# A 3x3 convolution: image pairs held whole, and output rows made in twos from a shared middle product

## The chip, the cores and the metric

The kernel runs on one core of a Trainium2 chip. The metric is device time in microseconds (us) from start to end of one execution. Three runs of the kernel before took 138.09, 137.21 and 137.68 us; the median is 137.68.

## The reference

The input x holds 16 images of 64 channels, 64 x 64 each, in fp32. The weight holds 128 output channels, 64 input channels and 3 x 3 taps; nine tenths of its values are zero, at places that follow no pattern. Each output pixel is the sum over input channels and taps, with a border of zeros around the image:

```python
x_pad = np.pad(x, ((0, 0), (0, 0), (pad, pad), (pad, pad)), mode='constant')
for b, co, ci, kh, kw in ...:
    if weight[co, ci, kh, kw] != 0:
        output[b, co] += weight[co, ci, kh, kw] * x_pad[b, ci, kh:kh+h, kw:kw+w]
```

The output is 16 x 128 x 64 x 64 in fp32, 33.55 MB; the input is 16.78 MB.

## The kernel before, in words

The convolution is done as matrix products: for one tap, the 64 x 128 matrix of its weights (input by output channels) times the pixels of some rows, shifted by the tap. The nine taps of a pixel are added up in one PSUM bank, which holds 512 fp32 values for each of 128 output channels, that is 8 rows of 64 pixels.

A product has only 64 input channels, so it fills half of TensorE's 128 rows of weights. The kernel splits each image: partitions 0 to 63 hold the channels of its upper 33 rows, partitions 64 to 127 those of its lower 33 rows (32 rows and the one that the middle tap row's neighbours need, XROWS = 33). One unit of work is 8 output rows in each half. It takes two PSUM tiles (psum_t, of 8 in the pool) and 18 matmuls, nine taps by two halves, the halves in turn (lines 151 to 181), so that two matmuls on different halves of the array can run beside each other. Pixels beyond the image's edge are left out of the matmul: 63 columns instead of 64 for the side taps, 7 rows instead of 8 at the top and the bottom.

Loads are issued by GpSimd, and they cast fp32 to bf16 on the way. Image 0 comes in four pieces (lines 54 to 60); images 1 to 14 in twos, one transfer for each half (lines 107 to 116), into three buffers, so that a load of a later group waits until TensorE is done with the buffer; image 15 in two transfers (lines 102 and 103).

The weights come by one load on SyncE's queue (line 64), VectorE casts them in three parts (line 70), TensorE multiplies them with an identity (made by GpSimd, line 76) to turn them, and ScalarE copies the result to wT, one 128 x 128 entry for each tap, with the same 64 rows in both halves (lines 79 to 91).

Finished PSUM tiles are copied to SBUF: for images 0 to 12 by VectorE or ScalarE as the planner picks (line 186; in the profile each gets one of the two), for images 13 to 15 by VectorE for the upper and ScalarE for the lower half (lines 188 and 191). Stores are issued by SyncE: images 0, 1 and 12 each by one transfer of 2 MB (line 202), images 2 to 11 in twos, 4 MB each (line 204), and images 13 to 15 in pieces of 512 KB as units finish, SyncE and ScalarE in turn (lines 197 and 199). The order of the instructions on each engine is the planner's, which takes the program's order as its priority.

Of the kernel before, what the change touches and what calls it, by code (L numbers as in the profile page):

```python
# [1 line left out]

# [5 lines left out]

FP32 = mybir.dt.float32  # L10
BF16 = mybir.dt.bfloat16


POS_ORDER = [(1, 1), (1, 0), (1, 2), (0, 0), (0, 1), (0, 2), (2, 0), (2, 1), (2, 2)]
CHUNK_ORDER = [1, 0, 2]


@with_exitstack
def kernel(
# [6 lines left out]
    nc = tc.nc  # L26

    B, C_IN, H, W = x.shape
    C_OUT, C_IN2, KH, KW = weight.shape
    assert (C_IN, H, W) == (64, 64, 64) and (C_OUT, KH, KW) == (128, 3, 3)  # L30

    HALF = H // 2
    XROWS = HALF + 1
    SPLIT = 10

    SINGLE_OUT = {0, 1, 12}
    PAIR_OUT_START = {2, 4, 6, 8, 10}
    STREAM_OUT = {13, 14, 15}
    UNITS_8 = [(r, 8) for r in range(0, HALF, 8)]
    STREAM_UNITS = {  # L40
        13: UNITS_8,
        14: UNITS_8,
        15: [(0, 8), (8, 8), (16, 8), (24, 4), (28, 4)],
    }
# [6 lines left out]
    psum_pool = ctx.enter_context(tc.tile_pool(name="psum", bufs=8, space=bass.MemoryType.PSUM))  # L51

    xs0 = x0_pool.tile([128, XROWS, W], BF16, name="xs0")
    nc.gpsimd.dma_start(out=xs0[0:64, 0:SPLIT], in_=x[0, :, 0:SPLIT, :])  # L54
    nc.gpsimd.dma_start(  # L55
        out=xs0[64:128, 0:SPLIT], in_=x[0, :, H - XROWS : H - XROWS + SPLIT, :]
    )
    nc.gpsimd.dma_start(out=xs0[0:64, SPLIT:XROWS], in_=x[0, :, SPLIT:XROWS, :])  # L58
    nc.gpsimd.dma_start(  # L59
        out=xs0[64:128, SPLIT:XROWS], in_=x[0, :, H - XROWS + SPLIT : H, :]  # L60
    )

    w_sb = const_pool.tile([C_OUT, C_IN * KH * KW], FP32)
    nc.sync.dma_start(out=w_sb, in_=weight.rearrange("o i kh kw -> o (i kh kw)"))
    w_sb3 = w_sb.rearrange("o (i k) -> o i k", k=KH * KW)

    w_bf = const_pool.tile([C_OUT, C_IN * KH * KW], BF16)
    w_bf3 = w_bf.rearrange("o (i k) -> o i k", k=KH * KW)
    for kh in CHUNK_ORDER:
        nc.vector.tensor_copy(  # L70
            out=w_bf3[:, :, kh * KW : (kh + 1) * KW],
            in_=w_sb3[:, :, kh * KW : (kh + 1) * KW],
        )

    ident = const_pool.tile([128, 128], BF16)
    make_identity(nc, ident)

    wT = const_pool.tile([128, KH * KW, C_OUT], BF16)
    for kh in CHUNK_ORDER:
        wps = psum_pool.tile([128, 4, 128], FP32, name="psum_t")  # L80
        for j in range(KW):
            sl = w_bf3[:, :, kh * KW + j]
            for half in range(2):
                nc.tensor.matmul(  # L84
                    wps[half * 64 : (half + 1) * 64, j, :],
                    sl,
                    ident,
                    start=True,
                    stop=True,
                )  # L90
        nc.scalar.copy(out=wT[:, kh * KW : kh * KW + KW, :], in_=wps[:, 0:KW, :])  # L91

    xs_group = None
    oimg_pair = None

    for b in range(B):
        if b == 0:
            xs = xs0
            xsel = ()
        elif b == B - 1:  # L100
            xs = x0_pool.tile([128, XROWS, W], BF16, name="xs15")
            nc.gpsimd.dma_start(out=xs[0:64], in_=x[b, :, 0:XROWS, :])  # L102
            nc.gpsimd.dma_start(out=xs[64:128], in_=x[b, :, H - XROWS : H, :])  # L103
            xsel = ()
        elif b % 2 == 1:
            xs_group = xg_pool.tile([128, 2, XROWS, W], BF16, name="xsg")
            nc.gpsimd.dma_start(  # L107
                out=xs_group[0:64].rearrange("i n r c -> i n (r c)"),
                in_=x[b : b + 2, :, 0:XROWS, :].rearrange("n i r c -> i n (r c)"),
            )  # L110
            nc.gpsimd.dma_start(  # L111
                out=xs_group[64:128].rearrange("i n r c -> i n (r c)"),
                in_=x[b : b + 2, :, H - XROWS : H, :].rearrange(
                    "n i r c -> i n (r c)"
                ),
            )
            xs = xs_group
            xsel = (0,)
        else:
            xs = xs_group  # L120
            xsel = (1,)

        if b in SINGLE_OUT or b in STREAM_OUT:
            oimg = outs_pool.tile([C_OUT, H, W], FP32, name="oimg")
        elif b in PAIR_OUT_START:
            oimg_pair = outg_pool.tile([C_OUT, 2, H, W], FP32, name="oimg2")
            oimg = oimg_pair[:, 0]
        else:
            oimg = oimg_pair[:, 1]

        streamed = b in STREAM_OUT
        if streamed:
            oimg_blk = oimg.rearrange("o (blk r) c -> o blk r c", blk=2)
            out_blk = out[b].rearrange("o (blk r) c -> o blk r c", blk=2)
            units = STREAM_UNITS[b]
        else:
            units = UNITS_8

        for ui, (ur0, rb) in enumerate(units):
            psums = []  # L140
            infos = []
            for half in range(2):
                r0 = half * HALF + ur0
                r1 = r0 + rb
                start_row = 0 if half == 0 else H - XROWS
                pbase = half * 64
                psum_t = psum_pool.tile([128, rb, W], FP32, name="psum_t")
                psums.append(psum_t)
                infos.append((r0, r1, start_row, pbase))

            for idx, (kh, kw) in enumerate(POS_ORDER):
                di, dj = kh - 1, kw - 1
                for half in range(2):
                    r0, r1, start_row, pbase = infos[half]
                    psum_t = psums[half]

                    i_lo = max(r0, -di)
                    i_hi = min(r1, H - di)
                    j_lo = max(0, -dj)
                    j_hi = min(W, W - dj)  # L160

                    rel_lo, rel_hi = i_lo - r0, i_hi - r0
                    xr_lo = i_lo + di - start_row
                    xr_hi = i_hi + di - start_row
                    xc_lo, xc_hi = j_lo + dj, j_hi + dj

                    idx_rhs = (slice(pbase, pbase + 64),) + xsel + (
                        slice(xr_lo, xr_hi),
                        slice(xc_lo, xc_hi),
                    )  # L170
                    rhs = xs[idx_rhs]
                    out_ap = psum_t[:, rel_lo:rel_hi, j_lo:j_hi]
                    lhsT = wT[pbase : pbase + 64, kh * KW + kw, :]

                    nc.tensor.matmul(  # L175
                        out_ap,
                        lhsT,
                        rhs,
                        start=(idx == 0),
                        stop=(idx == len(POS_ORDER) - 1),  # L180
                    )

            if not streamed:
                for half in range(2):
                    r0, r1, _, _ = infos[half]
                    nc.any.tensor_copy(out=oimg[:, r0:r1, :], in_=psums[half])  # L186
            else:
                nc.vector.tensor_copy(  # L188
                    out=oimg[:, infos[0][0] : infos[0][1], :], in_=psums[0]
                )  # L190
                nc.scalar.copy(  # L191
                    out=oimg[:, infos[1][0] : infos[1][1], :], in_=psums[1]
                )
                src = oimg_blk[:, :, ur0 : ur0 + rb, :]
                dst = out_blk[:, :, ur0 : ur0 + rb, :]
                if ui % 2 == 0:
                    nc.sync.dma_start(out=dst, in_=src)
                else:
                    nc.scalar.dma_start(out=dst, in_=src)  # L199

        if b in SINGLE_OUT:
            nc.sync.dma_start(out=out[b], in_=oimg)
        elif (b - 1) in PAIR_OUT_START:
            nc.sync.dma_start(
                out=out[b - 1 : b + 1].rearrange("n o h w -> o n (h w)"),
                in_=oimg_pair.rearrange("o n h w -> o n (h w)"),
            )


# [28 lines left out]
```

## Time and profile before

| what | value |
|---|---|
| median of three runs | 137.68 us |
| span of the profiled execution, first to last instruction | 136.1 us |
| TensorE busy with matmuls | 126.7 us (93%), 1188 of them |
| VectorE, ScalarE, GpSimd busy | 45.2, 40.2 and 12.2 us |
| last matmul ends | 130.5 us |
| read from and written to memory | 17.60 and 33.55 MB |
| TensorE's granted clock | 1.000 |

The profile is of one execution; its span runs from the first to the last instruction on the core, and the time measured for a run contains a little more than that. The page gives no other time of that execution, so its span is set beside the median of the runs. Engines are named PE (TensorE; PEld is its loading of weights), DVE (VectorE), ACT (ScalarE), POOL (GpSimd) and SP (SyncE); a q behind the name means the queue that issues transfers. In a row of the groups of instructions stand the line, the engine, the operation, the tiles written and read, the shapes, the count, then the busy time and the mean ns of one, then the engine's idle time just before and what ended it. In a row of stretches stand the stretch in us, its length, the busy time and count of PE, PEld, DVE, ACT and POOL, the granted clock, the mean busy share of the 16 DMA engines and the GB/s that they moved. A transfer that casts is counted there with the bytes that land. The share is the sum of the packets' times over the time of 16 engines, so it can pass 1 where packets overlap.

### The profile page before, as it was taken

The page shows a single profiled execution, that of the slowest core. Times are in us where ns is not written, and L with a number is a line of the kernel's source. Part 1 is how long each engine was busy: PE and PEld are TensorE (multiplying, and loading weights), DVE is VectorE, ACT ScalarE, POOL GpSimd, SP SyncE. Part 2 cuts the span into 40 slices and gives each one's busy share as a digit, 9 for nine tenths or more (in the row PEclk, how much of TensorE's full clock was granted, in tenths as well). Part 3 has the DMA queues.
Part 4 walks back from the last instruction along what each step waited for, and adds up shares of the span by engine and source line. Part 5 has one row for each costly group of instructions (what it writes and reads, how often), then busy time and mean ns, then how long its engine had stood idle before and what let it go on. Part 6 is the DMA issues. An engine that isn't in the chain of part 4 may idle for free.

```text
span 136.1 us, 2653 instructions
## 1 busy us (share of the span) xinstructions
PE 126.7 (93%) x1188; PEld 77.1 (57%) x1188; DVE 45.2 (33%) x68; ACT 40.2 (30%) x69; POOL 12.2 (9%) x26
## 2 busy tenths in 40 slices
PE   0699999999999999999999999999999999999960
PEld 0555666666565656665656655665656655656650
DVE  0203432344234432343234423443244333443240
ACT  3302332233323332233223332333233323332230
POOL 6950000003000110003000110000000000000000
PEclk9999999999999999999999999999999999999999
DMA  4999999999999999999999999999509999999884
GB/s 104 119 189 211 216 229 350 363 342 363 245 226 409 443 338 195 302 416 443 274 205 393 438 395 228 294 405 455 231 10 462 385 453 409 389 404 393 329 326 157
DMA packets 7980, 42.67 MB, mean 313 GB/s; under 512 B 673, under 2 KB 1313, under 8 KB 6305
## 3 DMA queue, kind: packets, MB, share of 16 engines
q1 hardware_dynamic: 3840, 30.97, 55.6%
q0 software_dynamic: 2496, 8.65, 33.4%
q10 hardware_dynamic: 1632, 2.88, 5.6%
q8 instruction: 9, 0.15, 0.4%
q14 instruction: 3, 0.02, 0.0%
HBM read 17.60 MB, written 33.55 MB: 376 GB/s over the span
## 4 chain that ended last, share of the span: by engine, by line
PE 92%; POOL 2%; issue 1%; ACT 1%; ACTq 0%; POOLq 0%
PE psum_t L175 91%; PE psum_t L84 1%; ACT oimg L191 1%; POOL xs L54 0%; ACTq L199 0%; POOL xs L55 0%; POOL xsg L107 0%; POOL xs L58 0%; POOL ident masks.py:199 0%; POOL ident masks.py:197 0%; POOL xs L59 0%; POOLq masks.py:199 0%; POOLq L222 0%
## 5 line engine op out<-in xcount | busy, mean ns | idle before, releaser
L175 PE MATMUL psum_t<-xsg,wT 64*128 64x512 bf16 (+2 forms) x1008 | 108.1, 374 | 0.0
L175 PEld LDWEIGHTS <-wT 64*128 64x128 bf16 x1170 | 75.8, 95 | 49.6 <-issue 1.9
L186 DVE COPY oimg<-psum_t 128x512 f32<-128x512 f32 x52 | 36.0, 692 | 68.6 <-PE psum_t L175 68.6
L186 ACT COPY oimg<-psum_t 128x512 f32<-128x512 f32 x52 | 30.5, 586 | 71.7 <-PE psum_t L175 71.7
L175 PE MATMUL psum_t<-xs,wT 64*128 64x504 bf16 (+5 forms) x162 | 18.0, 378 | 0.0
L188 DVE COPY oimg<-psum_t 128x512 f32<-128x512 f32 (+1 forms) x13 | 8.5, 650 | 14.3 <-PE psum_t L175 14.3
L191 ACT COPY oimg<-psum_t 128x512 f32<-128x512 f32 (+1 forms) x13 | 7.2, 554 | 16.0 <-PE psum_t L175 16.0
L107 POOL DMA_DIRECT2D xsg<-in_x_dram x7 | 4.2, 599 | 64.4 <-PE psum_t L175 64.4
L84 PE MATMUL psum_t<-ident,w_bf 128*64 128x128 bf16 x18 | 1.3, 321 | 4.7 <-POOL ident masks.py:199 4.7
L111 POOL DMA_DIRECT2D xsg<-in_x_dram x7 | 4.2, 607 | 0.0
L84 PEld LDWEIGHTS <-w_bf 128*64 128x64 bf16 x18 | 1.3, 208 | 4.5 <-DVE w_bf L70 4.1
L91 ACT CAST wT<-psum_t 128x384 bf16<-128x384 f32 x3 | 1.2, 487 | 3.3 <-PE psum_t L84 3.3
L70 DVE CAST w_bf<-w_sb 128x192 bf16<-128x192 f32 x3 | 0.8, 345 | 3.7 <-DMA w_sb<-in_weight_dram 3.7
L91 ACT ACT_TABLE_LOAD x1 | 1.3, 1283 | 0.7 <-PEq L222 0.7
L54 POOL DMA_DIRECT2D xs<-in_x_dram x1 | 0.7, 659 | 0.8 <-POOLq L222 0.8
L102 POOL DMA_DIRECT2D xs<-in_x_dram x1 | 0.5, 527 | 0.9 <-DMA xs<-in_x_dram 0.9
L103 POOL DMA_DIRECT2D xs<-in_x_dram x1 | 0.5, 522 | 0.4 <-DMA xs<-in_x_dram 0.4
L59 POOL DMA_DIRECT2D xs<-in_x_dram x1 | 0.6, 554 | 0.0
L55 POOL DMA_DIRECT2D xs<-in_x_dram x1 | 0.5, 542 | 0.0
L58 POOL DMA_DIRECT2D xs<-in_x_dram x1 | 0.5, 542 | 0.0
masks.py:199 POOL TENSOR_SCALAR_AFFINE_SELECT ident<-ident 128x128 bf16<-128x128 bf16 x1 | 0.4, 397 | 0.1
masks.py:197 POOL MEMSET ident<- 128x128 bf16 x1 | 0.3, 266 | 0.0
(4 smaller groups left out, 0.4 us busy)
## 6 DMA issues: line engine op xcount, KB each, us to landing
out_dram<-oimg SPq DMA_DIRECT2D x5, 4096.0 KB, 14.3
xsg<-in_x_dram POOLq DMA_DIRECT2D x14, 528.0 KB, 10.5
out_dram<-oimg SPq DMA_DIRECT2D x3, 2048.0 KB, 12.3
out_dram<-oimg SPq DMA_DIRECT2D x6, 512.0 KB, 7.0
out_dram<-oimg ACTq DMA_DIRECT2D x5, 512.0 KB, 6.8
xs<-in_x_dram POOLq DMA_DIRECT2D x2, 264.0 KB, 27.3
xs<-in_x_dram POOLq DMA_DIRECT2D x2, 184.0 KB, 6.0
w_sb<-in_weight_dram SPq DMA_DIRECT2D x1, 288.0 KB, 3.0
```

Source lines behind the costliest of these rows:

```text
L54: nc.gpsimd.dma_start(out=xs0[0:64, 0:SPLIT], in_=x[0, :, 0:SPLIT, :])
L55: nc.gpsimd.dma_start(out=xs0[64:128, 0:SPLIT], in_=x[0, :, H - XROWS : H - XROWS + SPLIT, :])
L59: nc.gpsimd.dma_start(out=xs0[64:128, SPLIT:XROWS], in_=x[0, :, H - XROWS + SPLIT : H, :])
L70: nc.vector.tensor_copy(out=w_bf3[:, :, kh * KW : (kh + 1) * KW], in_=w_sb3[:, :, kh * KW : (kh + 1) * KW],)
L84: nc.tensor.matmul(wps[half * 64 : (half + 1) * 64, j, :], sl, ident, start=True, stop=True,)
L91: nc.scalar.copy(out=wT[:, kh * KW : kh * KW + KW, :], in_=wps[:, 0:KW, :])
L107: nc.gpsimd.dma_start(out=xs_group[0:64].rearrange("i n r c -> i n (r c)"), in_=x[b : b + 2, :, 0:XROWS, :].rearrange("n i r c -> i n (r c)"),
L111: nc.gpsimd.dma_start(out=xs_group[64:128].rearrange("i n r c -> i n (r c)"), in_=x[b : b + 2, :, H - XROWS : H, :].rearrange("n i r c -> ...
L175: nc.tensor.matmul(out_ap, lhsT, rhs, start=(idx == 0), stop=(idx == len(POS_ORDER) - 1),)
L186: nc.any.tensor_copy(out=oimg[:, r0:r1, :], in_=psums[half])
L188: nc.vector.tensor_copy(out=oimg[:, infos[0][0] : infos[0][1], :], in_=psums[0])
L191: nc.scalar.copy(out=oimg[:, infos[1][0] : infos[1][1], :], in_=psums[1])
```

## The change

A pair of images now fills the partitions, one image's channels in 0 to 63 and the other's in 64 to 127, with all 64 rows. All eight pairs have a buffer of their own (x0 to x7), so all loads are issued at the beginning and none waits. Pair 0's first 9 rows come in fp32 by ScalarE's queue and are cast by ScalarE; its other rows by two casting loads; the other pairs by one each.

Output rows are made in twos. Let a, b, c be the three tap rows (above, middle, below) and x(r) the input rows. Row r of the output is a x(r-1) + b x(r) + c x(r+1), and row r+1 is a x(r) + b x(r+1) + c x(r+2). With the shared product P = b (x(r) + x(r+1)):

- row r = P + (c - b) x(r+1) + a x(r-1)
- row r+1 = P + (a - b) x(r) + c x(r+2)

That is five products by a tap row where there were six. A block in twos (function twos) is 16 output rows of both images. GpSimd adds the block's even and odd input rows into s (128 x 512, bf16). TensorE makes the shared product (3 taps by 2 images), then the even rows' (6 by 2) and the odd rows' (6 by 2), which read every second row of x. ScalarE copies the two shared results from PSUM to SBUF (pc), and VectorE adds them to the even and the odd results on the way from PSUM to the output tile, four additions of 128 x 512 in a block, each writing every second row.

Two blocks are still made directly, in units of 8 rows with nine taps: the first block of pair 0 and the last of pair 7. The tables of taps are now five groups of three: G1 (middle), G0 (above), G2 (below), G21 (below minus middle) and G01 (above minus middle); VectorE makes the two differences, after the first direct unit in the program's order. For each group three matmuls with the identity turn the weights.

Before the first real work TensorE runs seven matmuls on zeros. The whole body stands in a region in which every engine issues its instructions in the order of the program. The stores: pairs 0 to 6 by one transfer of 2 MB an image on SyncE's queue when the pair is done; pair 7 in two steps of 32 and 16 rows and two of 8 rows, the last ones on SyncE's and ScalarE's queues. Seven output tiles (o) of one image each go around.

The core of the diff, with lines of the kernel before as far as they are taken out around it:

```diff
-    x0_pool = ctx.enter_context(tc.tile_pool(name="x0", bufs=2))
-    xg_pool = ctx.enter_context(tc.tile_pool(name="xg", bufs=3))
-    outs_pool = ctx.enter_context(tc.tile_pool(name="osb", bufs=3))
-    outg_pool = ctx.enter_context(tc.tile_pool(name="osbg", bufs=2))
...
+BLOCKS = {p: "TTTT" for p in range(8)}
+BLOCKS[0] = "DTTT"
+BLOCKS[7] = "TTTD"
+G0, G1, G2, G21, G01 = range(5)
+KW_ORDER = (1, 0, 2)
...
+    HEAD = 9
+    CUT = 26
+    x_pool = ctx.enter_context(tc.tile_pool(name="x", bufs=1))
+    s_pool = ctx.enter_context(tc.tile_pool(name="s", bufs=3))
+    p_pool = ctx.enter_context(tc.tile_pool(name="pc", bufs=4))
+    o_pool = ctx.enter_context(tc.tile_pool(name="o", bufs=7))
...
+    ctx.enter_context(tc.manual_schedule())
...
+    nc.sync.dma_start(out=w_sb, in_=weight.rearrange("o i kh kw -> o (i kh kw)"))
+    nc.scalar.dma_start(out=x_head, in_=pair(0)[:, 0:HEAD, :])
+    nc.gpsimd.dma_start(out=xs[0][:, HEAD:CUT, :], in_=pair(0)[:, HEAD:CUT, :])
+    nc.gpsimd.dma_start(out=xs[0][:, CUT:H, :], in_=pair(0)[:, CUT:H, :])
+    ident = const_pool.tile([128, 128], BF16, name="ident")
+    make_identity(nc, ident)
+    for p in range(1, NP):
+        nc.gpsimd.dma_start(out=xs[p], in_=pair(p))
+    idle_rhs = const_pool.tile([128, 512], BF16, name="idle_rhs")
+    nc.vector.memset(idle_rhs, 0.0)
+    idle_ps = psum_pool.tile([128, 512], FP32, name="ps")
+    for _ in range(7):
+        nc.tensor.matmul(idle_ps, idle_rhs[:, 0:128], idle_rhs, start=True, stop=True)
+    nc.scalar.copy(out=xs[0][:, 0:HEAD, :], in_=x_head)
...
+    def transposed(g, copy):
+        wps = psum_pool.tile([128, 4, 128], FP32, name="ps")
+        for j in range(3):
+            src = w_bf[:, g, C_IN * j : C_IN * (j + 2)]
+            nc.tensor.matmul(wps[:, j, :], src, ident, start=True, stop=True)
+        copy(out=wT[:, g], in_=wps[:, 0:3, :])
+
+    for g in (G1, G0, G2):
+        for a, b in ((0, 3), (3, 4)):
+            k = 3 * g + a % 3
+            nc.vector.tensor_copy(out=w_bf4[:, g, a:b, :], in_=w_v[:, k : k + b - a, :])
+    transposed(G1, nc.scalar.copy)
+    transposed(G0, nc.vector.tensor_copy)
+    transposed(G2, nc.scalar.copy)
+
+    def differences():
+        for g, m in ((G21, 2), (G01, 0)):
+            for a, b in ((0, 3), (3, 4)):
+                k, k1 = 3 * m + a % 3, 3 + a % 3
+                nc.vector.tensor_tensor(
+                    out=w_bf4[:, g, a:b, :],
+                    in0=w_v[:, k : k + b - a, :],
+                    in1=w_v[:, k1 : k1 + b - a, :],
+                    op=SUB,
+                )
+            transposed(g, nc.scalar.copy)
+
+    def product(terms, rows):
+        ps = [psum_pool.tile([128, rows, W], FP32, name="ps") for _ in range(2)]
+        todo = [(t, kw) for t in terms for kw in KW_ORDER]
+        for i, ((src, g, first, step), kw) in enumerate(todo):
...
+            for n in range(2):
+                q = slice(64 * n, 64 * n + 64)
+                nc.tensor.matmul(
+                    ps[n][:, lo:hi, c_lo:c_hi],
+                    tap(g, kw, n),
+                    src[q, a:b:step, c_lo + kw - 1 : c_hi + kw - 1],
+                    start=(i == 0),
+                    stop=(i == len(todo) - 1),
+                )
+        return ps
+
+    def direct(p, o, r0, rows):
+        ps = product(
+            [(xs[p], G1, r0, 1), (xs[p], G0, r0 - 1, 1), (xs[p], G2, r0 + 1, 1)], rows
+        )
+        nc.scalar.copy(out=o[0][:, r0 : r0 + rows, :], in_=ps[0])
+        nc.vector.tensor_copy(out=o[1][:, r0 : r0 + rows, :], in_=ps[1])
+
+    def twos(p, o, r0):
+        t0 = r0 // 2
+        s = s_pool.tile([128, 8, W], BF16, name="s")
+        nc.gpsimd.tensor_tensor(
+            out=s, in0=xs[p][:, r0 : r0 + 16 : 2, :], in1=xs[p][:, r0 + 1 : r0 + 16 : 2, :], op=ADD
+        )
+        shared = product([(s, G1, 0, 1)], 8)
+        pc = []
+        for n in range(2):
+            c = p_pool.tile([128, 8, W], FP32, name="pc")
+            nc.scalar.copy(out=c, in_=shared[n])
+            pc.append(c)
+        even = [(xs[p], G21, r0 + 1, 2), (xs[p], G0, r0 - 1, 2)]
+        odd = [(xs[p], G01, r0, 2), (xs[p], G2, r0 + 2, 2)]
+        for first, terms in ((r0, even), (r0 + 1, odd)):
+            ps = product(terms, 8)
+            for n in range(2):
+                nc.vector.tensor_tensor(
+                    out=o[n][:, first : r0 + 16 : 2, :], in0=ps[n], in1=pc[n], op=ADD
                 )
...
+    for p in range(NP):
+        o = [o_pool.tile([C_OUT, H, W], FP32, name="o") for _ in range(2)]
+        last = p == NP - 1
+        for blk in range(4):
+            r0 = 16 * blk
+            if BLOCKS[p][blk] == "T":
+                twos(p, o, r0)
             else:
+                for r, rows in ((r0, 8), (r0 + 8, 8)):
+                    direct(p, o, r, rows)
+                    if p == 0 and blk == 0 and r == r0:
+                        differences()
+                    if last and blk == 3:
+                        nc.sync.dma_start(
+                            out=out[2 * p][:, r : r + rows, :], in_=o[0][:, r : r + rows, :]
+                        )
+                        nc.scalar.dma_start(
+                            out=out[2 * p + 1][:, r : r + rows, :], in_=o[1][:, r : r + rows, :]
+                        )
+            if last and blk in (1, 2):
+                a, b = (0, 32) if blk == 1 else (32, 48)
+                for n in range(2):
+                    nc.sync.dma_start(out=out[2 * p + n][:, a:b, :], in_=o[n][:, a:b, :])
+        if not last:
+            for n in range(2):
+                nc.sync.dma_start(out=out[2 * p + n], in_=o[n])
```

More of the change, by code (lines that the diff above doesn't have):

```diff
@@ L67 @@
[L67 to L72, printed above, removed]
-        )
[L75 to L89, printed above, removed]
-                )
-        nc.scalar.copy(out=wT[:, kh * KW : kh * KW + KW, :], in_=wps[:, 0:KW, :])
@@ L93 @@
[L93 to L186, printed above, removed]
-            else:
[L188 to L207, printed above, removed]
@@ new lines @@
+    C_OUT, _, KH, KW = weight.shape
+    assert (B, C_IN, H, W) == (16, 64, 64, 64) and (C_OUT, KH, KW) == (128, 3, 3)
+    NP = B // 2
+    HEAD = 9
+    CUT = 26
+    const_pool = ctx.enter_context(tc.tile_pool(name="const", bufs=1))
+    x_pool = ctx.enter_context(tc.tile_pool(name="x", bufs=1))
+    s_pool = ctx.enter_context(tc.tile_pool(name="s", bufs=3))
+    p_pool = ctx.enter_context(tc.tile_pool(name="pc", bufs=4))
+    o_pool = ctx.enter_context(tc.tile_pool(name="o", bufs=7))
+    psum_pool = ctx.enter_context(
+        tc.tile_pool(name="psum", bufs=8, space=bass.MemoryType.PSUM)
+    )
@@ new lines, with pair @@
+    ctx.enter_context(tc.manual_schedule())
+    def pair(p):
+        return x[2 * p : 2 * p + 2].rearrange("n i h w -> (n i) h w")
+    xs = [x_pool.tile([128, H, W], BF16, name=f"x{p}") for p in range(NP)]
+    w_sb = const_pool.tile([C_OUT, C_IN * KH * KW], FP32, name="w_sb")
+    x_head = const_pool.tile([128, HEAD, W], FP32, name="x_head")
+    nc.sync.dma_start(out=w_sb, in_=weight.rearrange("o i kh kw -> o (i kh kw)"))
+    nc.scalar.dma_start(out=x_head, in_=pair(0)[:, 0:HEAD, :])
+    nc.gpsimd.dma_start(out=xs[0][:, HEAD:CUT, :], in_=pair(0)[:, HEAD:CUT, :])
@@ new lines, with tap @@
+    nc.scalar.copy(out=xs[0][:, 0:HEAD, :], in_=x_head)
+    w_v = w_sb.rearrange("o (i k) -> o k i", k=KH * KW)
+    w_bf = const_pool.tile([C_OUT, 5, 4 * C_IN], BF16, name="w_bf")
+    w_bf4 = w_bf.rearrange("o g (k i) -> o g k i", k=4)
+    wT = const_pool.tile([128, 5, 3, C_OUT], BF16, name="wT")
+    def tap(g, kw, n):
+        return wT[64 * n : 64 * n + 64, g, (kw - n) % 3, :]
+    def transposed(g, copy):
[4 more added lines that the diff above has]
+        copy(out=wT[:, g], in_=wps[:, 0:3, :])
@@ new lines, in product @@
+    def product(terms, rows):
+        ps = [psum_pool.tile([128, rows, W], FP32, name="ps") for _ in range(2)]
+        todo = [(t, kw) for t in terms for kw in KW_ORDER]
+        for i, ((src, g, first, step), kw) in enumerate(todo):
+            n_src = src.shape[1]
+            lo = 0 if first >= 0 else 1
+            hi = rows if first + (rows - 1) * step < n_src else rows - 1
+            c_lo, c_hi = max(0, 1 - kw), min(W, W + 1 - kw)
+            a = first + lo * step
+            b = first + (hi - 1) * step + 1
+            for n in range(2):
[8 more added lines that the diff above has]
+        return ps
```

29 lines of the change are left out of this document (2 added, 27 removed).

## The prediction

> **What bounds the kernel now.** I read the page from the top: busy times, slices, queues, chain, groups.
>
> ```profile
> span 136.1 us, 2653 instructions
> PE 126.7 (93%) x1188; PEld 77.1 (57%) x1188; DVE 45.2 (33%) x68; ACT 40.2 (30%) x69; POOL 12.2 (9%) x26
> ...
> DMA  4999999999999999999999999999509999999884
> ...
> q1 hardware_dynamic: 3840, 30.97, 55.6%
> q0 software_dynamic: 2496, 8.65, 33.4%
> q10 hardware_dynamic: 1632, 2.88, 5.6%
> ...
> HBM read 17.60 MB, written 33.55 MB: 376 GB/s over the span
> ...
> PE 92%; POOL 2%; issue 1%; ACT 1%; ACTq 0%; POOLq 0%
> ...
> L186 DVE COPY oimg<-psum_t 128x512 f32<-128x512 f32 x52 | 36.0, 692 | 68.6 <-PE psum_t L175 68.6
> L186 ACT COPY oimg<-psum_t 128x512 f32<-128x512 f32 x52 | 30.5, 586 | 71.7 <-PE psum_t L175 71.7
> L107 POOL DMA_DIRECT2D xsg<-in_x_dram x7 | 4.2, 599 | 64.4 <-PE psum_t L175 64.4
> ...
> L91 ACT CAST wT<-psum_t 128x384 bf16<-128x384 f32 x3 | 1.2, 487 | 3.3 <-PE psum_t L84 3.3
> L70 DVE CAST w_bf<-w_sb 128x192 bf16<-128x192 f32 x3 | 0.8, 345 | 3.7 <-DMA w_sb<-in_weight_dram 3.7
> ...
> masks.py:199 POOL TENSOR_SCALAR_AFFINE_SELECT ident<-ident 128x128 bf16<-128x128 bf16 x1 | 0.4, 397 | 0.1
> masks.py:197 POOL MEMSET ident<- 128x128 bf16 x1 | 0.3, 266 | 0.0
> ...
> xsg<-in_x_dram POOLq DMA_DIRECT2D x14, 528.0 KB, 10.5
> ```
>
> TensorE is 93% busy and is 92% of the chain; VectorE and ScalarE wait for it (68.6 and 71.7 us). So TensorE is the bound. But the DMA row stands at 9 almost everywhere, and its queues add up to 55.6 + 33.4 + 5.6 = 94.6% of sixteen engines' span. The second limit is close behind the first, and how far decides this case. Stretches of the trace that hold one kind of transfer show it (columns: PE, PEld, DVE, ACT, POOL, granted clock, DMA share, GB/s):
>
> ```profile
> 0.00:2.00 2.00, 0.00 (x0) 0.00 (x0) 0.00 (x0) 1.26 (x1) 0.98 (x6) 1.00 0.16 24
> 6.00:10.00 4.00, 4.00 (x21) 1.96 (x23) 0.00 (x0) 0.68 (x3) 2.59 (x5) 1.00 1.02 180
> 10.00:20.00 10.00, 10.00 (x96) 6.02 (x94) 3.64 (x6) 3.22 (x6) 0.00 (x0) 1.00 1.07 215
> 60.00:70.00 10.00, 10.00 (x97) 6.04 (x94) 3.63 (x6) 3.27 (x6) 1.17 (x2) 1.00 1.00 338
> 90.00:96.00 6.00, 6.00 (x60) 3.62 (x58) 2.08 (x3) 1.76 (x3) 0.00 (x0) 1.00 1.02 434
> 96.00:102.00 6.00, 6.00 (x60) 3.62 (x58) 2.07 (x3) 1.76 (x3) 0.00 (x0) 1.00 0.22 93
> 102.00:128.00 26.00, 26.00 (x246) 15.64 (x244) 9.58 (x14) 8.01 (x14) 0.00 (x0) 1.00 1.01 408
> 134.00:136.00 2.00, 0.00 (x0) 0.00 (x0) 0.00 (x0) 0.00 (x0) 0.00 (x0) 1.00 0.12 31
> ```
>
> From 10 to 20 us nearly all traffic is loads: 215 GB/s with the engines full (1.07). Loads are counted in the bf16 that lands (528 KB is 64 partitions x 2 images x 33 rows x 64 columns x 2 bytes), so 430 GB/s of fp32 is read. From 90 to 96 us whole images are stored at 434 GB/s. From 102 to 128, mostly 512 KB stores, 408. From 96 to 102 the engines stand at 0.22 because all loads are done and no group of images is finished: there TensorE holds the DMA back. These are the rates at which the engines, full, stop going faster.
>
> **TensorE's term.** Per image, an 8-row unit has nine taps: 3 x 512 + 6 x 504 = 4560 columns, and 190 fewer in the top and bottom units (448 and 441 for three taps). 128 x 4560 - 32 x 190 = 577,600 columns in 1170 matmuls.
>
> ```profile
> 4.24 0.40 POOL ident masks.py:199
> 4.64 0.04 issue
> 4.69 1.30 PE psum_t L84 x18
> 5.99 124.54 PE psum_t L175 x1122
> ```
>
> They take 124.54 us, of which some is a slow beginning: 21 matmuls in 6:10 where 10:20 makes 38 in 4 us, so 17 x 0.106 = 1.8 us. The rest is 122.7 us, or 0.2125 ns a column (the two partition halves run together). After the change a 16-row block in twos has per image 15 products, 7,600 columns; 30 such blocks and two direct ones give 2 x (30 x 7,600 + 2 x 9,120) - 32 x 190 = 486,400 columns in 972 matmuls: 103.4 us, 19.3 fewer. A block in twos takes 15,200 columns, 3.23 us; a direct one 3.88. The seven idle products pay the slow beginning while the weights are on their way; without that cover 1.8 us return.
>
> Matmuls start near 5.3 us instead of 5.99. The identity stands behind two load issues instead of five, so weights come last: landed at 3.7, two casts of the first group (345 ns for 192 elements, about 0.2 for 64) to 4.3, three transposing products at 1.30 / 18 = 0.07 us, ScalarE's copy 0.49, and the latencies between. Ahead of that copy in ScalarE's queue stand the head's load issue and its cast (576 elements, some 0.65 by 586 for 512), which ends as the products do; if the head lands late, the start moves with it. New is a wait. Instructions keep the written order on every engine, so the products that transpose the two difference tables (G21, G01) stand in TensorE's queue between the first two direct units. They need VectorE's subtractions, which stand behind its copy of the first unit's result. First unit 1.9 us, to 7.2; copy 0.69 to 8.0; four subtractions. At the casts' 0.35 and 0.2 they take 1.1 us (twice that if two inputs cost double), with the last transposes and ScalarE's copies to 9.4. TensorE stands for 2.2 us, up to 3.3; the second direct unit queues behind it. So it ends at 5.3 + 103.4 + 2.2 = 110.9 us.
>
> **What stands beside it.** A shorter copy gives VectorE's slope.
>
> ```profile
> L188 DVE COPY oimg<-psum_t 128x256 f32<-128x256 f32 x2 | 0.8, 424 | 0.9 <-PE psum_t L175 0.9
> ```
>
> Per block in twos (3.23 us) VectorE has four adds of 128x512. No row adds two tensors. Below stands the copy, 692 ns. Above: 256 elements more cost 692 - 424 = 268 ns, so 156 ns fixed and 536 for 512 elements; two inputs read in turn make 156 + 2 x 536 = 1228. I take 692, since one input comes from PSUM and one from SBUF: 4 x 0.692 = 2.77 us, inside 3.23. ScalarE's two copies are 2 x 0.586 = 1.17. GpSimd makes one sum of 128x512 bf16: four times the 266 ns of the 128x128 memset is 1.1 us, four times the 397 of the select 1.6, double that for two inputs 3.2. I take 1.6, the one that reads; with three buffers it runs ahead. Its nine load issues, at 599 ns, come first (until about 7 us), and the first sum is wanted at 11.5.
>
> **DMA's term.** Loads are 64 rows an image instead of 66: 8.39 MB of bf16, less the 9 of pair 0's 64 rows that go another way (1.8%): 8.24 / 0.215 = 38.3 us. Stores 33.55 MB / 0.434 = 77.3 us. Weights and the fp32 head are 0.59 MB: 1.4 us at 408 GB/s. At both ends the engines are empty: 2 x (1 - 0.16) + 2 x (1 - 0.12) = 3.4 us. Sum 120.4 us, if they never run dry between. So by the rows 434 GB/s written and 430 read. [...]
>
> Do they? All loads are issued in the first 7 us and nothing holds them (the 64.4 us at L107 goes). They fill the engines alone until pair 0's images are done (near 22 us), then share with stores. By then 20 of 38 us of loads are through, some three and a half pairs; pair 4 lands by about 34 and is wanted at 59, so the load wait does not return as a wait on TensorE. The seven output buffers are no wait either: pair 4 needs pair 1's first image stored, about 50 us against 59, and later pairs have over 8 us. Pair 6 is finished at 110.9 - (3 x 3.23 + 3.88) = 97.3 plus two adds, 98.8 us; from there two pairs' stores remain, 8.39 / 0.434 = 19.3 us, and 1.8 of the empty end: 119.9. The route by TensorE (119.9) and the route by DMA (120.4) meet. The DMA engines become the bound, and about 4 of TensorE's gain stay unused. Span 120.4; the median of the three runs stands 137.68 - 136.1 = 1.6 us over the profiled span, so **122.0 us**.
>
> **Rivals.** (1) *The DMA engines are slower than those clean stretches.* Stores at the 408 of 102:128 cost 82.2, 4.9 more: 126.9. If every packet costs what its queue's row shows and none overlap, 94.6% of 136.1 = 128.8 us, less 1.4 (2 of 66 rows of the loads' 45.5), plus 0.8 for the head's second pass at small rows and 3.4: 131.6, or 133. For it: mixed stretches show 1.00 (60:70). Against: a share of 1.07 says packet times overlap.
>
> (2) *DMA keeps ahead*, and TensorE stays the bound: 110.9 plus before's tail, 136.1 - 130.5 (5.99 + 124.54) = 5.6: 116.5, or 118.1. That needs stores well over 434 GB/s, which none of the stretches above shows.
>
> (3) *VectorE becomes the bound, and the kernel slower.* The place is the four adds of each block. TensorE hides up to 3.23 / 4 = 0.81 us each; beyond that it waits for a PSUM buffer. Start, stall, direct blocks, less the edge rows, and tail make 19.6 us, so 19.6 + 30 b = 136.1 at b = 3.88: from 0.97 us an add the kernel is slower than now. At the 1228 bound b is 4.9 and the time 168. Against it only that the two inputs lie in different memories. GpSimd's sum would do the same above 3.9 us, beyond its upper bound of 3.2.
>
> (4) *No change: the products aren't worth what they count.* 12 of a block's 15 read every second row, which no row of this trace does. If they cost a quarter more, 96.9 x 0.8 x 0.25 = 19.4 us, the gain is undone: 137 to 138. For it, nothing; against it, only that 64 and 63 columns of a row lie together as before.
>
> (5) *Memory caps loads and stores together, and the kernel is slower.* If the mean of 376 GB/s is all that memory gives while the engines run, 2 x 8.39 + 0.29 + 33.55 = 50.6 MB take 134.6 us and with the empty ends 138.0, or 139.6. Against it: 430 read in 10:20, 434 written in 90:96, and a mean that holds the hole of 96:102. [...]
>
> **Numbers.** Forecast (119.5 to 126) 0.66; rival 1 beyond 126 0.14; rival 2 0.10; rival 4 0.03; rival 3 0.05; rival 5 0.02. The range 118 to 130 holds the forecast with both store rates, most of rival 2 and half of rival 1; outside are its rest and the cases of no gain. One per cent is what a measurement can tell here. Faster: 0.66 + 0.14 + 0.10 = 0.90; same 0.03; slower 0.07.
>
> **What would show it.** DMA share near 1 from 2 us to the end, without the hole of 96:102; TensorE's share at about 104 of 120, with idle time late in the span only if output buffers run out; the chain ending in stores, not in TensorE. VectorE's adds near 0.7 us and GpSimd's sums between 1.1 and 1.6; a TensorE gap near 2 us at the differences. I am wrong if matmuls wait on PSUM buffers in every block (rival 3), if the pitch of matmuls on stepped rows exceeds 0.106 us (rival 4), or if stores of whole images run under 400 GB/s (rival 1).

## The result and the profile after

The changed kernel takes 132.5 us (median of four runs, 130.78 to 132.87), where the kernel before takes 137.87 (four runs now): the ratio is 0.9587, with a 95% interval of 0.9518 to 0.9657. The ratio leaves out the longest run of the changed kernel, which counts as slow. It is faster, as forecast, but by 5.4 us and not by 15.7, and 132.5 lies outside the range of 118 to 130. The profiled execution took 132.56 us with a span of 130.8.

The page of the changed kernel, the lines that answer to those shown of before:

```profile
span 130.8 us, 2474 instructions
PE 113.5 (87%) x994; PEld 49.5 (38%) x994; DVE 84.0 (64%) x136; ACT 38.4 (29%) x70; POOL 40.5 (31%) x45
...
PE   6692699999999999999999999999999999994000
...
PEclk9999559999999999999999999999999999999655
DMA  4999999999999999999999999999599929989991
...
q1 hardware_dynamic: 3024, 33.33, 61.1%
q0 software_dynamic: 1296, 8.24, 31.0%
q10 hardware_dynamic: 432, 0.82, 1.8%
...
PE 84%; DVE 4%; DMA 3%; issue 0%
...
L166 DVE TENSOR_TENSOR o<-ps,pc 128x512 f32<-128x512 f32 x120 | 75.3, 686 | 22.3 <-PE ps L133 20.0
L152 POOL TENSOR_TENSOR s<-x 128x512 bf16<-128x512 bf16 x30 | 34.8, 1164 | 61.9 <-PE ps L133 47.6
```

VectorE's adds (line 166) take 686 ns and GpSimd's sums (line 152) 1164: neither is a bound. Three other things stand in these lines. TensorE's row has a hole in its fourth slice, at 10 to 13 us. The granted clock falls to about half in the two slices of 13 to 20 us (0.51 over that stretch; the lower digits at the row's end come after the last matmul); in the kernel before it read 1.00 all through. And the DMA row, forecast full to the end, has a 5 and a 2 late in the span.

The chain of waits of the changed kernel, in order of time (start, length, what), shows the beginning:

```profile
0.74 4.19 DMA w_sb<-in_weight_dram
...
5.50 1.55 PE ps L95 x9
7.06 3.27 PE ps L133 x18
...
10.35 0.69 DVE o L147
11.04 3.29 DVE w_bf L110 x3
...
14.38 0.50 PE ps L95 x3
14.88 104.48 PE ps L133 x954
```

The first direct unit starts at 7.06 us and takes 3.27; then come VectorE's copy and 3.3 us of subtractions (line 110), and TensorE goes on at 14.88. It ends at 119.36, where 110.9 was forecast. Stretches of the same trace, with the columns of the prediction's:

```profile
15.00:20.00 5.00, 5.00 (x26) 1.76 (x24) 0.69 (x1) 0.98 (x2) 0.00 (x0) 0.52 1.04 216
92.00:96.00 4.00, 4.00 (x42) 1.82 (x38) 3.42 (x6) 1.07 (x2) 1.15 (x1) 1.00 0.59 244
104.00:108.00 4.00, 4.00 (x42) 1.83 (x40) 2.69 (x6) 1.57 (x4) 0.68 (x1) 1.00 0.25 98
```

Between 15 and 20 us TensorE makes 26 matmuls at a clock of 0.52, about half of its usual 48 to 50. Near 93 and 105 us the DMA engines run dry (shares of 0.59 and 0.25), because no pair is finished; together they lose 4.6 us there.

The subtractions stand in the groups of the changed kernel, shapes kept apart:

```profile
L110 DVE TENSOR_TENSOR w_bf<-w_sb 128x192 bf16<-128x192 f32 x2 | 2.3, 1149 | 0.0
L110 DVE TENSOR_TENSOR w_bf<-w_sb 128x64 bf16<-128x64 f32 x2 | 1.5, 738 | 0.0
L101 DVE CAST w_bf<-w_sb 128x192 bf16<-128x192 f32 x3 | 1.5, 492 | 3.8 <-DMA w_sb<-in_weight_dram 3.8
```

1149 and 738 ns, where 0.35 and 0.2 us were put in. GpSimd's first three sums run just then, from 10.30 to 13.96 us:

```profile
10.30 3.66 POOL L152 TENSOR_TENSOR s<-x 128x512 bf16<-128x512 bf16 x3 [2.34 <-DMA x<-in_x_dram]
10.96 3.54 DVE L110 TENSOR_TENSOR w_bf<-w_sb 128x192 bf16<-128x192 f32 x4
```

The means hide how large the difference is. The view of line 110 by itself gives the shortest, the median and the longest of the four in ns:

```profile
L110 DVE TENSOR_TENSOR w_bf<-w_sb x4: 259/1035/1445, 11.0 to 14.2; 128x192 bf16<-128x192 f32 x2, 128x64 bf16<-128x64 f32 x2
```

With the two means, that makes 853 and 1445 ns for the two of 192 elements, and 1217 and 259 for the two of 64. The 259 belongs to the last one, which starts when the sums are over.

### The profile page after: what moved, and what is told of

Its sections match the earlier page's. It is cut to its first block, busy times and chain, and to the rows that moved or that the text cites. A ratio compares the mean times of both kernels' runs of the same rounds, so it can differ in the third digit from the quotient of the medians.

```text
span 130.8 us, 2474 instructions
## 1 busy us (share of the span) xinstructions
PE 113.5 (87%) x994; PEld 49.5 (38%) x994; DVE 84.0 (64%) x136; ACT 38.4 (29%) x70; POOL 40.5 (31%) x45
## 4 chain that ended last, share of the span: by engine, by line
PE 84%; DVE 4%; DMA 3%; issue 0%
PE ps L133 82%; DMA w_sb<-in_weight_dram 3%; DVE w_bf L110 3%; PE ps L95 2%; DVE o L147 1%; DVE w_bf L101 0%
## 5 line engine op out<-in xcount | busy, mean ns | idle before, releaser
L133 PE MATMUL ps<-x,wT 64*128 64x504 bf16 (+3 forms) x792 | 92.7, 383 | 0.0
L166 DVE TENSOR_TENSOR o<-ps,pc 128x512 f32<-128x512 f32 x120 | 75.3, 686 | 22.3 <-PE ps L133 20.0
L133 PEld LDWEIGHTS <-wT 64*128 64x128 bf16 x972 | 47.5, 96 | 59.7 <-issue 4.8
L152 POOL TENSOR_TENSOR s<-x 128x512 bf16<-128x512 bf16 x30 | 34.8, 1164 | 61.9 <-PE ps L133 47.6
L159 ACT COPY pc<-ps 128x512 f32<-128x512 f32 x60 | 32.2, 589 | 62.4 <-issue 59.6
L133 PE MATMUL ps<-s,wT 64*128 64x512 bf16 (+1 forms) x180 | 24.9, 384 | 0.0
L147 DVE COPY o<-ps 128x512 f32<-128x512 f32 x4 | 2.8, 692 | 9.1 <-PE ps L133 9.1
L77 PE MATMUL ps<-idle_rhs 128*128 128x512 bf16 x7 | 3.2, 630 | 1.2 <-DVE idle_rhs L74 1.2
L70 POOL DMA_DIRECT2D x<-in_x_dram x7 | 3.7, 553 | 1.2 <-DMA x<-in_x_dram 1.2
L110 DVE TENSOR_TENSOR w_bf<-w_sb 128x192 bf16<-128x192 f32 (+1 forms) x4 | 3.5, 944 | 0.0
L65 POOL DMA_DIRECT2D x<-in_x_dram x1 | 0.7, 693 | 0.8 <-POOLq L210 0.8
L66 POOL DMA_DIRECT2D x<-in_x_dram x1 | 0.5, 536 | 0.0
```

Source lines behind the costliest of these rows:

```text
L70: nc.gpsimd.dma_start(out=xs[p], in_=pair(p))
L77: nc.tensor.matmul(idle_ps, idle_rhs[:, 0:128], idle_rhs, start=True, stop=True)
L110: nc.vector.tensor_tensor(out=w_bf4[:, g, a:b, :], in0=w_v[:, k : k + b - a, :], in1=w_v[:, k1 : k1 + b - a, :], op=SUB,)
L133: nc.tensor.matmul(ps[n][:, lo:hi, c_lo:c_hi], tap(g, kw, n), src[q, a:b:step, c_lo + kw - 1 : c_hi + kw - 1], start=(i == 0), stop=(i == ...
L147: nc.vector.tensor_copy(out=o[1][:, r0 : r0 + rows, :], in_=ps[1])
L152: nc.gpsimd.tensor_tensor(out=s, in0=xs[p][:, r0 : r0 + 16 : 2, :], in1=xs[p][:, r0 + 1 : r0 + 16 : 2, :], op=ADD)
```

## The experiments

The theory after the result has three parts. (a) GpSimd's sums hold up the subtractions, which makes the hole long. (b) The hole lets the clock fall, which costs as much again. (c) The late pairs let the DMA engines run dry, and with that gone the DMA engines are the bound, at more than was forecast.

**e1_fill: idle products in the hole.**

```diff
+    def fill(n):
+        t = psum_pool.tile([128, 512], FP32, name="ps")
+        for _ in range(n):
+            nc.tensor.matmul(t, idle_rhs[:, 0:128], idle_rhs, start=True, stop=True)
...
     def differences():
         for g, m in ((G21, 2), (G01, 0)):
+            fill(7 if g == G21 else 5)
```

> Undisturbed order, but idle products on zeros stand in TensorE's queue where it waits for the two difference tables (7 ahead of G21's transposes, 5 ahead of G01's). Theory A (the clock falls because TensorE stands still for 4.5 us; the 2.9 us that the second direct unit and the first block lose after it come from that): the granted clock stays at 1.00 through 10 to 20 us, the hole itself stays, TensorE ends near 116.5 us instead of 119.4, and the time falls by 2.9 to about 129.6. Rival B (the clock falls at that point whatever TensorE does): clock near 0.5 from 12 to 20 us as before, time 132.5.

It takes 128.7 us (ratio to before 0.939, interval 0.933 to 0.945). Its trace, chain and one stretch:

```profile
6.49 2.02 PE ps L139 x18
...
13.44 102.04 PE ps L139 x954
```

```profile
15.00:20.00 5.00, 5.00 (x50) 2.25 (x46) 3.15 (x5) 2.25 (x5) 1.59 (x2) 1.00 1.02 213
```

The hole is still 4.9 us (8.51 to 13.44), but the clock reads 1.00 and the 954 matmuls behind it take 102.04 us instead of 104.48. So the clock falls because TensorE stands still: 2.4 us. Here the weights also came half a microsecond earlier and the first unit ran at full rate (2.02 us), which the fill, standing behind both, cannot have caused; that is why TensorE ends at 115.5 and not at 116.5, and the time gains more than forecast.

**e2_early: subtractions ahead of the first unit's copy.**

```diff
-    def differences():
+    def subtract():
...
+    def differences():
+        for g in (G21, G01):
+            transposed(g, nc.scalar.copy)
+    subtract()
```

> The four subtractions stand on VectorE ahead of the copy of the first direct unit, so that they run before GpSimd's first sum; the transposes keep their place on TensorE. Theory A (two SBUF inputs on VectorE and GpSimd's two-input sums hold each other up): the subtractions take 0.36 us (192 elements) and 0.2 us (64) instead of 1.15 and 0.74, 1.1 us together; TensorE's hole shrinks from 4.5 to about 0.5 us, the clock stays at 1.00 behind it, TensorE ends near 112.5 us, time about 125.5. Rival B (subtractions of two strided fp32 inputs cost that much by themselves): 1.15 and 0.74 us each again, 3.5 us together, with a hole of about 1 us.

127.59 us, ratio 0.929 (0.925 to 0.933). The subtractions, by shapes:

```profile
L110 DVE TENSOR_TENSOR w_bf<-w_sb 128x192 bf16<-128x192 f32 x2 | 1.0, 491 | 0.0
L110 DVE TENSOR_TENSOR w_bf<-w_sb 128x64 bf16<-128x64 f32 x2 | 0.5, 263 | 0.0
```

Before GpSimd's first sum they take 491 and 263 ns, 1.26 us in all. The hole is 0.4 us and the clock stays at 1.00. TensorE ends at 112.45, as theory A had it, yet the time is 2.1 us above its 125.5: the tail behind TensorE's end is now 13.2 us long. The DMA row and the stretches say why:

```profile
DMA  3999999999999999999999999999999999999990
```

```profile
0.00:5.00 5.00, 3.17 (x7) 0.89 (x7) 0.81 (x4) 1.64 (x2) 3.89 (x12) 1.00 0.65 161
5.00:25.00 20.00, 19.93 (x171) 8.99 (x173) 12.64 (x26) 7.50 (x15) 9.69 (x11) 1.00 1.05 216
25.00:30.00 5.00, 5.00 (x50) 2.25 (x46) 4.11 (x7) 1.83 (x4) 1.81 (x2) 1.00 1.01 256
30.00:60.00 30.00, 30.00 (x286) 13.70 (x282) 23.16 (x37) 9.98 (x19) 10.85 (x10) 1.00 1.02 321
60.00:110.00 50.00, 50.00 (x472) 22.92 (x470) 39.33 (x64) 16.10 (x30) 13.82 (x12) 1.00 1.01 428
110.00:120.00 10.00, 2.41 (x24) 0.92 (x20) 1.63 (x3) 1.17 (x2) 0.00 (x0) 0.76 0.99 411
120.00:125.70 5.70, 0.00 (x0) 0.00 (x0) 0.00 (x0) 0.00 (x0) 0.00 (x0) 0.50 0.45 178
```

The engines are full from 5 to 120 us and still need 125.7. If this is the DMA bound of the prediction, it lies 5.3 us above the size that it was given; e7_cut, further down, tests that it is one.

**e3_direct: every block made directly.**

```diff
-BLOCKS = {p: "TTTT" for p in range(8)}
-BLOCKS[0] = "DTTT"
-BLOCKS[7] = "TTTD"
+BLOCKS = {p: "DDDD" for p in range(8)}
```

> Every block is made directly with nine taps, so no sums on GpSimd, no shared products and no adds of two tensors; pairs resident, stores and start as in the changed kernel. Theory A (the five-for-six saving is worth its 19.3 us on TensorE, and the subtractions are slowed by GpSimd's sums): the same beginning but subtractions of 0.36 and 0.2 us, hole near 2.2 us; TensorE needs 122.7 us at full clock and ends at about 134 to 137; time 140 to 144, slower than the kernel before. Rival B (holding pairs gave the gain, or products on every second row cost more than others): time near 133 or below.

144.86 us, ratio 1.051 (1.042 to 1.060), 12.4 us above the changed kernel. Its chain, and the same subtractions at the same place of VectorE's order, now with no sums on GpSimd:

```profile
12.88 121.49 PE ps L131 x1134
```

```profile
L108 DVE TENSOR_TENSOR w_bf<-w_sb 128x192 bf16<-128x192 f32 x2 | 1.0, 492 | 0.0
L108 DVE TENSOR_TENSOR w_bf<-w_sb 128x64 bf16<-128x64 f32 x2 | 0.5, 267 | 0.0
```

Behind the hole TensorE needs 121.49 us where blocks in twos need 102.04 at full clock: 19.45 us are what five products for six are worth on TensorE, against 19.3 forecast, and products on every second row cost no more than others. The time came out just above the 140 to 144 expected. Pairs held whole are by themselves no gain: with them, nine taps and this beginning, the kernel is slower than before.

**e9_blank: GpSimd's sums later, with everything else in its order.**

```diff
+    blank = const_pool.tile([128, 512], FP32, name="blank")
+    for _ in range(12):
+        nc.gpsimd.memset(blank, 0.0)
```

> The changed kernel in its own order, but GpSimd fills a spare tile with zeros twelve times (it writes and reads nothing) between its load issues and its first sum, so that the sums come after the subtractions. Theory A (GpSimd's sums, which read SBUF, hold the subtractions up): 0.49 and 0.26 us a subtraction, 1.3 us together instead of 3.5; TensorE's hole 2.3 us instead of 4.5, and with the shorter hole a clock dip that is smaller or gone; TensorE ends between 114.5 and 117, time 128 to 130. Rival B (any work on GpSimd does it, or the subtractions are slow at that moment for another reason, such as transfers): 1.15 and 0.74 us again and 132.5.

128.13 us, ratio 0.931 (0.927 to 0.935). GpSimd is busy with the zeros from 6.74 to 13.69 us, and the subtractions in that time take:

```profile
L113 DVE TENSOR_TENSOR w_bf<-w_sb 128x192 bf16<-128x192 f32 x2 | 1.0, 492 | 0.0
L113 DVE TENSOR_TENSOR w_bf<-w_sb 128x64 bf16<-128x64 f32 x2 | 0.5, 262 | 0.0
```

```profile
PEclk9999999999999999999999999999999999999555
```

So it is not GpSimd's being busy, nor the transfers (their share from 10 to 15 us is 1.04 here and 1.03 in the changed kernel), but the sums. The sums read SBUF and the zeros do not; no run here separates the reading from whatever else sets a sum apart. With the short hole (2.2 us) the clock does not fall either, and TensorE ends at 115.0. The zeros make GpSimd's first sum late, and TensorE waits 2.1 us for it; that costs some of the gain.

**e4_warm: 13 idle products at the beginning.**

```diff
-    for _ in range(7):
+    for _ in range(13):
```

> 13 idle products on zeros at the beginning instead of 7. Theory A (the first direct unit ran at half rate because TensorE stood still from 4.4 to 5.5 us and had not been busy for long enough): the first unit takes 1.9 us instead of 3.3, and TensorE ends 1.2 us earlier; time about 131.3. Rival B (the first unit is slow for another reason, such as its taps being read for the first time): still 3.3 us, time 132.5 or a little more.

131.06 us, in runs from 128.04 to 131.9, too spread for an interval. The chain of its trace says what the expectation asked:

```profile
1.19 4.71 PE ps L77 x13
...
6.63 2.08 PE ps L133 x18
...
13.50 104.46 PE ps L133 x954
```

The idle products now reach to 5.9 us, and the first unit takes 2.08 us instead of 3.27. The hole and the half clock behind it are there as before (104.46). One trace would not show that the thirteen did it, for seven sometimes do as well. Over all traces: with seven the first unit took 2.02 to 2.04 us in three (e1_fill, e6_halves, e9_blank) and 3.0 to 3.8 in four (the changed kernel, e2_early, e3_direct, e7_cut); with thirteen it took 2.04 to 2.08 in all three (e4_warm, e5_early_warm, e8_tail). Seven are not enough to be sure of it; thirteen look like it, on three traces.

**e6_halves: pairs 4 to 6 stored in halves.**

```diff
+            if 4 <= p < NP - 1 and blk in (1, 3):
+                a, b = (0, 32) if blk == 1 else (32, 64)
+                for n in range(2):
+                    nc.sync.dma_start(out=out[2 * p + n][:, a:b, :], in_=o[n][:, a:b, :])
...
-        if not last:
+        if not last and p < 4:
```

> The changed kernel with its late beginning as it is, but pairs 4 to 6 are stored in halves of 32 rows (1 MB an image) as these are done. Theory A (the late beginning costs time only because whole pairs are stored: the DMA engines run dry at 92 to 96 and 104 to 108 us, 4.7 us together): the holes close, TensorE still ends near 119.4 us and the time falls to 127.5 to 129. Rival B (the late TensorE itself sets the end, through the last pair): 131 to 132.5.

128.87 us, ratio 0.937 (0.932 to 0.942). The same two stretches:

```profile
92.00:96.00 4.00, 4.00 (x42) 1.78 (x40) 3.17 (x6) 1.91 (x4) 1.91 (x2) 1.00 1.01 426
104.00:108.00 4.00, 4.00 (x42) 1.78 (x40) 3.42 (x7) 1.11 (x3) 0.00 (x0) 1.00 1.01 422
```

Both holes of the DMA engines are closed, with the long hole of TensorE (4.2 us) and its half clock left in (0.56 from 13 to 19 us). TensorE ended at 117.6 here, 1.8 us earlier than in the changed kernel's profile, its first unit being quicker; 3.6 us of time are more than that. The four runs have mean granted clocks of 0.947, 0.953, 0.968 and 0.970 and yet lie within 0.22 us of each other, which suggests that the time no longer follows TensorE. So most of what the late beginning costs, it costs because whole pairs are stored and the DMA engines have nothing to do in between. Not all: 1.3 us remain to e2_early.

The same trace holds the clearest view of the sums and the subtractions, because here two subtractions ran before the first sum and two beside the sums:

```profile
L110 DVE TENSOR_TENSOR w_bf<-w_sb x4: 262/854/1458, 9.4 to 11.3; 128x192 bf16<-128x192 f32 x2, 128x64 bf16<-128x64 f32 x2
```

The first took 489 ns (192 elements) and 262 (64), the second two 1458 and 1219.

**e5_early_warm: e2_early with 13 idle products.**

> Early subtractions and 13 idle products together. Theory A (with the subtractions early the DMA engines are the bound from the beginning to the end, full in every slice): TensorE ends 1.4 us earlier, near 111 us, and the time stays at 127.6, within 0.5. Rival B (the time still follows TensorE's end): 126.2.

127.45 us, ratio 0.927 (0.924 to 0.930), the same as e2_early. TensorE ended only 0.5 us earlier (111.98) and not 1.4, because the thirteen products held it until 6.72 us, so this run alone would not have told much; the next one does.

**e7_cut: e2_early without a fifth of the work of most blocks.**

```diff
-        odd = [(xs[p], G01, r0, 2), (xs[p], G2, r0 + 2, 2)]
+        odd = [(xs[p], G01, r0, 2)]
```

> Early subtractions, and the odd rows of every block in twos leave out the products with the tap row below (G2): 180 of 972 matmuls are gone, so part of the output lacks a third of its sum. TensorE ends about 19 us earlier, near 93. Theory A (the DMA engines bound the kernel at 50.6 MB / 0.424 = 119.4 us plus some 6 us of empty ends): the time stays at 126.5 to 127.6. Rival B (TensorE or the work behind it still decides): 115 to 122.

126.65 us, ratio 0.921 (0.917 to 0.925). The rows of its page and a part of its chain:

```profile
PE 93.6 (75%) x814; PEld 43.5 (35%) x814; DVE 80.7 (65%) x136; ACT 38.2 (31%) x70; POOL 40.1 (32%) x45
...
DMA  3999999999999999999999999999999999999991
```

```profile
41.85 27.82 DMA out_dram<-o
```

TensorE is rid of 17 us of work, and the time falls by 0.9. The DMA engines are full all the way. TensorE, running ahead, has to wait for a store that frees an output buffer (it ends at 99.8, not at 93 as I had expected). So the 125.7 us of e2_early are a bound by the DMA engines: faster matrix work is worth next to nothing here any more.

**e8_tail: e5_early_warm with pair 7's last block in twos and its last 16 rows in one store an image.**

```diff
-BLOCKS[7] = "TTTD"
...
-            if last and blk in (1, 2):
-                a, b = (0, 32) if blk == 1 else (32, 48)
+            if last and blk in (1, 2, 3):
+                a, b = {1: (0, 32), 2: (32, 48), 3: (48, 64)}[blk]
```

> Early subtractions, 13 idle products, and pair 7's last block in twos too, its last 16 rows stored by one transfer an image (4 KB rows) instead of two (2 KB rows). Theory A (only the DMA engines count; 2 x 84 - 159 = 9 ns a row pair over 256 rows on 16 engines is 0.14 us): 127.3 to 127.6, no gain that can be told. Rival B (the last small stores hold the end up): 126 to 127.

127.59 us, ratio 0.928 (0.924 to 0.932): no difference from e5_early_warm. e2_early, e5_early_warm and e8_tail beat both kernels, by about 10 us the kernel before and by about 5 the changed one.

## Why the prediction was wrong, and where it was right

**TensorE's term: right.** 101.5 us were forecast for what follows the first unit, 102.04 is measured at full clock (e1_fill, e2_early); the difference to nine taps is 19.45 us (e3_direct) against 19.3. Rival 4 falls.

**The start at 5.3: mis-sized by 1.8 us.** The weights landed at 4.93 us and not at 3.7: their load took 4.19 us where it took 3.0 before. The head's load is now under way beside it, but no run leaves that out, so the reason is open. The other 0.5 us lie between the landing and the first unit, 2.13 us instead of 1.6. The prediction counted one group's casts and products there; in fact all nine products stand ahead of the first unit, paced by six casts (4.95 to 6.62 us), and a cast of 192 took 492 ns instead of 345 (it now reads every ninth value of the weights where it read them in threes; whether that is why, no run tests).

**The cover by idle products: failed.** They end at 4.36 us, the first real product starts at 5.50, and the first unit ran for 3.27 us instead of 1.9: 1.4 us. That is partly a matter of luck, as the count in e4_warm shows. The gap does not decide it by itself: TensorE stood for 0.68 us in e1_fill and for 0.66 in e2_early, and the first units took 2.02 and 3.40. What decides it stays open.

**The wait at the differences: its place right, its size wrong.** 2.2 us were put in, with 3.3 as the upper bound; the hole is 4.55 us (10.33 to 14.88). The bound came from VectorE's own rows. What was left out is that the first sums, which with three buffers run ahead, would run against the subtractions. e9_blank and e3_direct show it: 1.3 us without the sums, 3.5 with them. The sums lose by it too: of thirty, the longest took 1401 ns and the median 1154. The subtractions, with both inputs in SBUF, took 1458 and 1219 ns beside sums (e6_halves) and 492 and 262 beside zeros (e9_blank); the changed kernel's 120 adds, with one input in PSUM, took 680 to 693 although a sum runs in every block. Why sums and subtractions slow each other is not shown.

**What the prediction did not have at all: the clock behind the hole.** The stretch of 15 to 20 us has a granted clock of 0.52, and the same 954 matmuls take 104.48 us instead of 102.04; with the 0.54 by which TensorE's own term was short, that is 2.98 over the 101.5. I had priced the hole by its length alone. Holes of 4.55 (changed kernel), 4.8 (e4_warm) and 4.2 us (e6_halves), with only a few short transposing products in them, had the lower clock behind them: 0.52 and 0.66 from 15 to 20 us, and 0.56 from 13 to 19. Behind holes of 2.2 us (e3_direct, e9_blank) it read 1.00, as it did behind one of 4.9 us with idle products in it (e1_fill). Between 2.2 and 4.2 us no run has a hole, so what length of hole brings the fall is not shown here.

Together, start, first unit, hole and what follows: 1.76 + 1.37 + 2.35 + 2.98 = 8.46 us, which is TensorE's end at 119.36 instead of 110.9.

**That the DMA engines never run dry between: failed, through the above.** The prediction saw the two routes meet, within half a microsecond, at 119.9 and 120.4, and so had nothing in hand. Pair 6's stores were issued at 107.3 instead of 98.8, and before them and before pair 5's the DMA engines ran dry. e6_halves shows that the late TensorE matters mostly because whole pairs are stored. The span of 130.8 is thus 120.4 + 5.3 + 5.1: 5.3 by which the DMA bound was too small (next paragraph), and 5.1 over the 125.7 of e2_early, of which 4.6 are the two holes.

**The DMA term: right in kind, 5.3 us too small.** That DMA bounds the kernel once TensorE is out of the way is shown by e7_cut. Its size is 125.7 (e2_early) instead of 120.4. By an estimate from the stretches shown there, priced with the prediction's own rates (215 and 434): both ends cost some 6.0 us instead of 3.4, for reasons that no run here takes apart; 25 to 30, where the stores begin, loses 0.7; the last stores in short rows (411) 0.55; and from 30 to 110 us the rates lie a little lower, 1.2 us. I had taken the best stretch of six microseconds for the rate of a hundred.

**Rivals 1 and 2.** Rival 1's two numbers came close by luck. Its 126.9 us, from stores at 408 GB/s, lies near the 127.6 of e2_early, but there the stores ran at 428 for 50 us, and the ends cost more. Its sum without overlap, 131.6 in the span, lies near the 130.8 measured, but e2_early moves the same bytes in 125.7. Rival 2, DMA keeping ahead, is refuted: with TensorE ending at 112.45 in e2_early, the stores go on for 13 us.

**Rivals 3 and 5: refuted.** The adds take 686 ns, where 692 to 1228 were given. Memory gives more than 376 GB/s: e2_early runs loads at 216 landed, 432 read, and stores at 428 GB/s for 50 us.

None of the prediction's three signs of being wrong came up: no wait on PSUM buffers in every block, the same 0.107 us a matmul on stepped rows (e1_fill) as on whole ones (e3_direct), whole images stored at over 400 GB/s. These signs watch the steady state; the prediction failed at the beginning and at the ends.

## What to carry to other kernels

When two bounds meet within a microsecond, nothing hides a delay at the beginning: of the 6.9 us by which TensorE ended later here than in e2_early, 4.9 came out in the time. So price the first 15 us row by row, with what each engine's neighbour does at that moment. Subtractions on VectorE with both inputs in SBUF took 1.26 us in all ahead of GpSimd's sums (e2_early) and 3.54 where the sums ran beside them (changed kernel), so such work is worth keeping away from the sums. TensorE's hole of 4.55 us was paid twice here, in its length and in 2.4 us by the clock behind it; idle products in it kept the clock at 1.00 (e1_fill), and moving what it waits for ahead left 0.4 us of it (e2_early). And pairs stored in halves gave the DMA engines work sooner with TensorE late: shares of 1.01 where they were 0.59 and 0.25 (e6_halves).

## What was not expected of the hardware

In e6_halves a subtraction of 128 x 64 with two SBUF inputs took 262 ns alone and 1219 beside GpSimd's sums, one of 128 x 192 489 and 1458. The granted clock read 1.00 during the first unit of the changed kernel, where 18 matmuls took 3.27 us, against 2.02 in e1_fill; it showed the fall from 15 to 20 us (0.52), not the slow beginning. And the DMA engines moved nearly the same whichever way the data went: 216 GB/s landed, 432 read, in loads alone, 428 in stores alone. Between 5 and 120 us of e2_early that comes to some 48.6 of the kernel's 50.6 MB, or 423 GB/s; all of them would take about 120 us by this estimate, without the empty ends.
